# Hybrid decoder layer on one Trainium2 core: operand sums on VectorE alone and over four buffers, gate additions issued behind weight sums, and a new order for the last up-projection unit and the accumulators

## The chip, the cores and the metric

The kernel runs on one NeuronCore of a Trainium2 chip. The metric is the device time of one execution in microseconds. The kernel before took 2260.38 us, the median of three runs (2256.8 to 2262.14).

## The reference, cut to what matters

```python
h = rms_norm(x, norm_mix_g)
proj = h @ w_in                       # q, k, v, gates of three branches
y_m = sigmoid(mo) * rms_norm(mlstm_chunkwise(...))      # branch M
y_d = diff_attention(...)                               # branch D
y_c = memory_cross_attention(cq, mem, ...)              # branch C
g_m, g_d, g_c = split(sigmoid(h @ w_gate + b_gate), 3)
merged = g_m * (y_m @ w_proj_m) + g_d * (y_d @ w_proj_d) + g_c * (y_c @ w_proj_c)
x = x + merged @ w_out
h2 = rms_norm(x, norm_mlp_g)
x = x + square(relu(h2 @ w_up)) @ w_down
```

There are 1024 positions, a width of 1024 and a hidden width of 4096, all in float32. The change concerns the last five lines: the three branch projections with their gates, the output projection and the MLP.

## The kernel before

**First half.** The norm of x, branch C, branch M and branch D are computed one after the other, and the gate columns in pieces between and beside them. A gate step is three matmuls. Each branch writes its result y to device memory, and the gates go there too (line 474).

**Matrix products.** Every product is three matmuls of a high and a low part of the two operands (`mm3`): a source is split into `hi`, a cast on ScalarE, and `lo`, the source less that, on VectorE.

**The stream.** From `stream()` on, the three branch projections, the up and the down projection run as Strassen-Winograd products: a block of weights (four pieces) is summed to seven by four additions on GpSimd (`wino_s`, tiles `wraw`), then split (`wo`); a block of operands (four pieces) is summed to seven in the same way (`wino_t` or `x_fold`), then split (`xo`); seven products of them, 21 matmuls of 128x512, make one weight step n; four steps accumulate in seven PSUM banks and make a round. The steps are numbered through: 0 to 15 are branch C (four rounds), 16 to 31 branch M, 32 to 47 branch D, 48 to 59 the output projection (plain products, tiles `po`), 60 to 123 the up projection (16 rounds, units u), 124 to 187 the down projection (16 rounds p). There are eight banks and a round takes seven, so the first product of a round uses the free one and each later product waits until a sum of the round before has read its bank. These sums (`sums`: one copy on ScalarE, seven additions on VectorE into `c11`, `c21`, `u3`, `u2`, shown as c and u) make the four output blocks.

**Order.** In the stream ScalarE, VectorE, GpSimd and SyncE run in the order of the program text. After each step `side(n)` issues `w_next(n + 3)`, which is the weight sums of what was loaded last (GpSimd), the next weight loads (SyncE) and the split of weight n + 3 (ScalarE, VectorE), and then all that the table `todo` holds for step n, in the order of its list. So whatever waits holds up all that is behind it on its engine.

**Operand sums ahead of the stream.** `x_jobs` (lines 1141 to 1170) makes the operands of branches C, M and D from their y: a job is a pair of rows of blocks and makes two items; an item loads half a tile `xj` (two loads, SyncE), makes three sums on VectorE and one on GpSimd (line 1137), and stores the result to `xtC_d`, `xtM_d` or `xtD_d`, or splits it at once. It is a generator, advanced once per gate step: it waits `wait[0]` steps between the load of an item and the sums of the item before, and `wait[1]` steps up to the store. Three jobs run beside the 64 gate steps between M and D, with waits (4, 5); nine run beside the 96 gate steps ahead of the stream, with waits (3, 4) and three buffers; what is left when the gate steps end is issued behind them. The stream starts with loads of two more operand tiles (`xo`) of branch C.

**Gates.** `fetch` loads a gate block (`gl`), `gate` multiplies (1 + gate) by an output block on VectorE, and GpSimd adds the product to the merged block `mg` (branch M) or the other way about (branch D). In branch M blocks 1, 3 and 2 are done at the round's end n and block 0 at n + 1 or n + 2, since it comes after the load of its gate. The blocks c11, c21 and the gates share a ring of five buffers.

**The second norm** is computed within the first up rounds: `rstd` issues small matmuls (`px`) into the free bank at three points, given by `mid`. `use_up` applies the norm, ReLU and square to an up round's blocks (VectorE, two ScalarE activations for each of four blocks); `up_rest` makes their operand sums (`xts`) and `up_store` stores them (`r_d`). **Down rounds** accumulate in 28 tiles `acc`, loaded with x at step 126 from `x_d`, which lie over the memory of pools closed before (`accum`).

Of the kernel before, what the change touches and what calls it, by code (L numbers as in the profile page):

```python
# [71 lines left out]
class Layer:  # L72
# [1068 lines left out]
    def x_jobs(self, pool, jobs, wait):  # L1141

        V, G = self.nc.vector, self.nc.gpsimd
        items = [(s, kp, slice(c, c + 256)) for s, kp in jobs for c in (0, 256)]
        tiles = []
        for i in range(len(items) + 1):
# [9 lines left out]
            if i:  # L1156
                s, kp, c = items[i - 1]
                r = tiles.pop(0)
                x = self.X[s, kp] if s == "C" and kp < 2 else None
                if x is not None:  # L1160
                    self.split(x[:, 0, 0:3, c], x[:, 1, 0:3, c], r[:, 1:4])
                self.wino_t(r, r, V, G)
            for _ in range(wait[1]):
# [150 lines left out]
    def stream(self):  # L1314
# [33 lines left out]
        def gate(s, u, cs, *order):  # L1348
            for i in order:
                t, k = tg[i], (2 * u + i // 2, i % 2)  # L1350
                if s == "C":
                    mg[k] = mlp.tile([P, 512], F32, tag="ml", name=self.name("mg"))
                V.scalar_tensor_tensor(
                    out=mg[k] if s == "C" else t, in0=t, scalar=1.0, in1=cs[i], op0=ALU.add, op1=ALU.mult
                )
                if s == "M":
                    G.tensor_add(mg[k], mg[k], t)
                elif s == "D":
                    (V if u == 3 else G).tensor_add(t, mg[k], t)
# [60 lines left out]
        for r in range(12):  # L1420
            s, u = "CMD"[r // 4], r % 4
            ps = run(r, (0, 1, 2, 3), s, n)
            n += 4
            cs = sums(ps, four())
            if s == "D":
                if u < 3:
                    gate(s, u, cs, 1, 3, 2, 0)
                    side(n)
                    todo.setdefault(n + 1, []).insert(0, lambda u=u: operands(u, 1, 3, 2, 0))
                continue  # L1430
            m = n + 2 if u == 3 else n
            todo.setdefault(m, []).insert(0, lambda s=s, u=u, cs=cs: gate(s, u, cs, 1, 3, 2))
            m = max(m, n + 1)
            todo.setdefault(m, []).insert(m > n + 1, lambda s=s, u=u: fetch(s, u, 0))
            todo.setdefault(m + 1, []).insert(0, lambda s=s, u=u, cs=cs: gate(s, u, cs, 0))
            side(n)
        self.w_next(n + 3)
        extra.close()
        T["hj"] = R("mhj", his, 2)
        gate("D", 3, cs, 1)  # L1440
        operands(3, 1)
        fetch("D", 3, 0)
        gate("D", 3, cs, 3, 2)
        operands(3, 3, 2)
        gate("D", 3, cs, 0)
        operands(3, 0)
        left.close()
# [11 lines left out]
        def result(u, ps):  # L1459
            x = T["x"]  # L1460
            b = T["b"] = T["o"].tile([P, 4, 512], F32, tag="o", name=self.name("h2"))
            for i in range(4):
                s = slice(i % 2 * 512, (i % 2 + 1) * 512)
                V.scalar_tensor_tensor(out=x[:, i], in0=ps[i], scalar=0.5, in1=x[:, i], op0=ALU.mult, op1=ALU.add)
                v = R_MLP + 2 * u + i // 2
                A.activation(b[:, i], x[:, i], AF.Copy, scale=self.vec[:, v : v + 1])
                if u == 0 and i < 2:
# [11 lines left out]
        for g in range(4):  # L1479
            ps = [pw.tile([P, 512], F32, tag=f"p{4 * (g % 2) + i}", name=self.name("po")) for i in range(4)]  # L1480
            for c in range(3):
# [7 lines left out]
                if c < 2:  # L1489
                    side(n)  # L1490
            result(g, ps)
            if g == 3:
# [29 lines left out]
        next(rs)  # L1522
        mid = {(62, 3): rs.send, (63, 3): rs.send, (64, 2): rs.send}

# [13 lines left out]

        def up_store():
            S.dma_start(*T["rd"])  # L1540

        for u in range(16):
            m = 126 if u == 15 else 64 + 4 * u + (u == 0)
            at(m, up_rest, u)
            at(m + (u < 15), up_store)
        at(110, self.x_load, "N", 0)
# [11 lines left out]
        def accum():  # L1558
            left.close()
            lp = L("acc")  # L1560
            accs.extend(lp.tile([P, 512], F32, name=f"acc{i}") for i in range(28))

# [7 lines left out]
        for u in range(16):  # L1570
# [6 lines left out]
            else:  # L1577
                todo.setdefault(64 if u == 0 else 125, []).insert(0, lambda u=u, cs=cs: use_up(u, cs))
            for f in todo.pop(n, []):
# [69 lines left out]
    def run(self):  # L1649
        tc, nc = self.tc, self.nc  # L1650
        with ExitStack() as ctx:
# [22 lines left out]
            with ExitStack() as c1:  # L1674
# [143 lines left out]
```

## Time and profile before

| What | Value |
|---|---|
| median of 3 runs | 2260.38 us (2256.8 to 2262.14) |
| the profiled execution | 2260.53 us |
| its span, first to last instruction | 2258.8 us |
| mean granted TensorE clock | 0.983 |
| TensorE busy | 95% of the span |
| VectorE, ScalarE, GpSimd busy | 67%, 45%, 26% |
| stream begins | at 1221.48 us |

The profile comes from one execution. A row of a timeline gives the start, the duration, the engine, the operation with its output and inputs, how many were merged, and in brackets the idle time before and what ended it. A row of waits gives the total, how often, and the longest. A row of the windows gives the stretch, its length, busy time with the number of instructions of each engine (TensorE, its weight loads, VectorE, ScalarE, GpSimd), the granted TensorE clock, the mean busy share of the 16 DMA engines, and GB/s. Line 67 is the helper through which the stream issues all its instructions, and line 93 the one for matmuls, so the tiles' names tell what an instruction is. PE is TensorE, DVE VectorE, ACT ScalarE, POOL GpSimd, SP SyncE.

### The profile page before, as it was taken

What the parts mean: (1) busy time and instruction counts of PE and PEld (TensorE: products, weight loads), DVE (VectorE), ACT (ScalarE), POOL (GpSimd) and SP (SyncE); (2) the same over time, 40 slices, a digit from 0 to 9 for tenths busy, and PEclk for the clock granted to TensorE, in tenths of its full rate; (3) what the DMA queues carried; (4) which work ended last, traced back from release to release, by engine and by line L of the source; (5) the groups of instructions that cost most, each with busy time, mean ns of one, the idle gap of its engine ahead of it and who ended that gap; (6) DMA issues with size and microseconds to landing.
All of it is one profiled execution on the core that took longest, in us unless ns stands there. A gap on an engine that the chain in (4) does not pass through costs nothing. (4 is left out here: it accounts for less than half of the span.)

```text
span 2258.8 us, 30482 instructions
## 1 busy us (share of the span) xinstructions
PE 2156.7 (95%) x10953; PEld 1841.5 (82%) x10953; DVE 1516.9 (67%) x2764; ACT 1021.1 (45%) x1995; POOL 591.1 (26%) x568
## 2 busy tenths in 40 slices
PE   7999999999999999999998899899999999699998
PEld 5888888988899999999876667678778887588886
DVE  6643565655347777777644787986688877666687
ACT  6543455444246666665531332324344445443332
POOL 2100000000111111111022347742544434344441
PEclk9999999999999999999999899899999999899999
DMA  7023222121643333333349555334244455554433
GB/s 245 29 85 108 64 83 80 43 71 38 221 117 89 94 89 86 86 85 89 86 148 297 201 182 185 136 103 145 78 145 154 154 186 184 222 200 154 154 137 143
DMA packets 138398, 293.51 MB, mean 130 GB/s; under 512 B 13793, under 2 KB 44806, under 8 KB 132486
## 3 DMA queue, kind: packets, MB, share of 16 engines
q1 hardware_dynamic: 135942, 278.98, 37.9%
q10 hardware_dynamic: 2304, 12.58, 1.4%
q8 instruction: 86, 1.41, 0.3%
q14 instruction: 66, 0.54, 0.1%
HBM read 192.91 MB, written 73.43 MB: 118 GB/s over the span
## 5 line engine op out<-in xcount | busy, mean ns | idle before, releaser
L93 PE MATMUL p<-xo,wo 128*128 128x512 f32 x3696 | 873.8, 398 | 63.4 <-ACT xo L67 22.2
L93 PEld LDWEIGHTS p<-xo,wo 128*128 128x128 f32 x3696 | 703.0, 192 | 232.6 <-ACT xo L67 23.8
L93 PE MATMUL mm<-w,hT 128*128 128x384 f32 (+3 forms) x2496 | 472.2, 331 | 8.9 <-DVE dsg L114 5.5
L67 POOL TENSOR_TENSOR wraw<-wraw 128x256 f32<-128x256 f32 x352 | 374.9, 1076 | 358.0 <-DMA wraw<-in_wdown 148.1
L93 PE MATMUL mm<-hT,w 128*128 128x512 f32 x1920 | 466.4, 395 | 1.9 <-ACT gt L473 1.2
L93 PEld LDWEIGHTS mm<-hT,w 128*128 128x128 f32 x1920 | 353.2, 188 | 77.1 <-ACT gt L473 2.4
L93 PEld LDWEIGHTS mm<-w,hT 128*128 128x128 f32 x2496 | 388.2, 189 | 22.8 <-DVE dsg L114 7.7
L67 ACT CAST wo<-wraw 128x896 fp32r<-128x896 f32 (+1 forms) x186 | 171.2, 931 | 445.2 <-PE p L93 222.5
L67 DVE TENSOR_TENSOR wo<-wraw,wo 128x896 fp32r<-128x896 f32 (+1 forms) x186 | 232.1, 1254 | 171.0 <-ACT wo L67 170.3
L114 DVE TENSOR_TENSOR w<-raw,w 128x256 fp32r<-128x256 f32 (+3 forms) x272 | 130.5, 502 | 60.2 <-ACT w L113 59.4
L1009 ACT ACTIVATE dpe<-sc,dst,drr 128x256 f32<-128x256 f32 (+7 forms) x128 | 106.6, 833 | 99.8 <-DVE dst L1005 91.1
L113 ACT CAST w<-raw 128x256 fp32r<-128x256 f32 (+3 forms) x272 | 121.5, 469 | 66.2 <-PE mm L93 26.3
L67 DVE TENSOR_TENSOR xo<-xo 128x1536 fp32r<-128x1536 f32 (+1 forms) x58 | 127.1, 2207 | 20.8 <-ACT xo L67 19.8
L129 POOL TENSOR_SCALAR hss<-hss 128x4 f32<-128x4 f32 x8 | 3.3, 408 | 414.4 <-ACT mscr L754 273.1
L67 ACT CAST xo<-xo 128x1536 fp32r<-128x1536 f32 (+1 forms) x58 | 97.0, 1691 | 25.7 <-DMA xo<-y 21.4
L1001 DVE CUSTOM_DVE_ANT_0 sc<-sc,tmask 128x256 f32<-128x256 f32 (+7 forms) x128 | 97.1, 758 | 12.7 <-PE sc L93 12.6
L67 DVE TENSOR_TENSOR u<-u,p 128x512 f32<-128x512 f32 x140 | 93.8, 686 | 12.7 <-DVE c L67 0.9
L93 PE MATMUL sc<-dk,dq 128*128 128x512 f32 (+3 forms) x384 | 90.3, 343 | 0.0
L129 POOL TENSOR_SCALAR drr<-drr 128x16 f32<-128x16 f32 x16 | 3.3, 204 | 313.4 <-DVE drr L955 313.4
L93 PE MATMUL po<-mh,wo 128*128 128x512 f32 x256 | 79.0, 389 | 0.0
L93 PE MATMUL po<-dv,daT 128*128 128x256 f32 x576 | 75.2, 274 | 0.5 <-DVE daT L114 0.5
L93 PEld LDWEIGHTS po<-dv,daT 128*128 128x128 f32 x576 | 74.0, 189 | 1.6 <-DVE daT L114 0.9
(267 smaller groups left out, 2450.9 us busy)
## 6 DMA issues: line engine op xcount, KB each, us to landing
xo<-r_d SPq DMA_DIRECT2D x19, 1024.0 KB, 6.7
dk<-dsg SPq DMA_DIRECT2D x64, 256.0 KB, 4.4
wraw<-in_wup SPq DMA_DIRECT2D x64, 256.0 KB, 3.5
r_d<-xts SPq DMA_DIRECT2D x16, 1024.0 KB, 4.4
wraw<-in_wdown SPq DMA_DIRECT2D x64, 256.0 KB, 4.0
xo<-r_d SPq DMA_DIRECT2D x19, 768.0 KB, 4.4
raw<-in_wgate SPq DMA_DIRECT2D x48, 256.0 KB, 3.2
gates<-gt SPq DMA_DIRECT2D x48, 256.0 KB, 3.3
```

Source lines behind the costliest of these rows:

```text
L67: return self.tc.keep_in_program_order(f(*a, **k))
L93: self.pin(self.nc.tensor.matmul(out, l, r, start=start, stop=stop))
L113: nc.scalar.copy(hi, src)
L114: nc.vector.tensor_sub(lo, src, f32(hi))
L129: g.tensor_scalar(r, ss, 1.0 / width, EPS, op0=ALU.mult, op1=ALU.add)
L1001: V.tensor_tensor_reduce(out=sc[:, 0:n], in0=sc[:, 0:n], in1=self.tmask[:, D - n : D], scale=1.0, scalar=-3.0e38, op0=ALU.add, op1=ALU.max ...
L1009: nc.scalar.activation(pe[c][:, 0:n], sc[:, 0:n], AF.Exp, bias=t8[:, 2 + c : 3 + c], scale=rr[:, i, c : c + 1], accum_out=t8[:, 4 + c : 5 ...
```

## The change

1. `x_jobs` makes all four sums of an item on VectorE (`x_fold`). One M job moves from the last gate stage to the one between M and D (8 and 16 items now instead of 6 and 18). The waits become (3, 4) in the former and (2, 4) in the latter, which has four buffers instead of three.
2. The additions behind the gates become a function of their own (`adds`). In branch M (rounds 0 to 2) they are issued one step after the gate product, behind the weight sums of that step, and block 0's gate load, product and addition one step later than before. In branch D (rounds 0 to 2) the gate product is issued behind the weight split of its step instead of ahead, the addition one step later, and the split of the merged block (`operands`) at the third step instead of the first.
3. In the output projection, four casts come ahead of four squares, and `w_sums` is called ahead of `result`.
4. The second and third point of the norm's small matmuls move from steps (63, 3) and (64, 2) to (64, 0) and (64, 4); unit 0's `use_up` and `up_rest` come one step later.
5. Unit 15's `use_up` comes behind the operand split of step 125 instead of ahead, its `up_store` is issued from GpSimd instead of SyncE, and the 28 accumulators lie in reverse order in memory, so that the first round's seven lie over pools closed long before rather than over the buffers of `xts`.

```diff
-                self.wino_t(r, r, V, G)
+                self.x_fold(r, r, V)
...
-                if s == "M":
-                    G.tensor_add(mg[k], mg[k], t)
-                elif s == "D":
+        def adds(s, u, *order):
+            for i in order:
+                t, k = tg[i], (2 * u + i // 2, i % 2)
+                if s == "M":
+                    G.tensor_add(mg[k], mg[k], t)
+                else:
                     (V if u == 3 else G).tensor_add(t, mg[k], t)
...
+            put = lambda m, f, *x: todo.setdefault(m, []).insert(0, lambda: f(*x))
             if s == "D":
                 if u < 3:
-                    gate(s, u, cs, 1, 3, 2, 0)
+                    put(n + 3, operands, u, 1, 3, 2, 0)
+                    put(n + 1, adds, s, u, 1, 3, 2, 0)
+                    put(n, gate, s, u, cs, 1, 3, 2, 0)
                     side(n)
-                    todo.setdefault(n + 1, []).insert(0, lambda u=u: operands(u, 1, 3, 2, 0))
                 continue
+            late = s == "M" and u < 3
             m = n + 2 if u == 3 else n
-            todo.setdefault(m, []).insert(0, lambda s=s, u=u, cs=cs: gate(s, u, cs, 1, 3, 2))
-            m = max(m, n + 1)
-            todo.setdefault(m, []).insert(m > n + 1, lambda s=s, u=u: fetch(s, u, 0))
-            todo.setdefault(m + 1, []).insert(0, lambda s=s, u=u, cs=cs: gate(s, u, cs, 0))
+            if s == "M":
+                put(m + late, adds, s, u, 1, 3, 2)
+            if u == 3:
+                todo.setdefault(m, []).insert(s == "M", lambda s=s, u=u: fetch(s, u, 0))
+            else:
+                at(n + 1 + late, fetch, s, u, 0)
+            put(m, gate, s, u, cs, 1, 3, 2)
+            e = m + 1 if u == 3 else n + 2 + late
+            if s == "M":
+                put(e, adds, s, u, 0)
+            put(e, gate, s, u, cs, 0)
             side(n)
...
-        mid = {(62, 3): rs.send, (63, 3): rs.send, (64, 2): rs.send}
+        mid = {(62, 3): rs.send, (64, 0): rs.send, (64, 4): rs.send}
...
-            m = 126 if u == 15 else 64 + 4 * u + (u == 0)
+            m = 126 if u == 15 else 64 + 4 * u + 2 * (u == 0)
             at(m, up_rest, u)
-            at(m + (u < 15), up_store)
+            at(m + (u < 15), up_store, S if u < 15 else G)
...
-            accs.extend(lp.tile([P, 512], F32, name=f"acc{i}") for i in range(28))
+            accs.extend([lp.tile([P, 512], F32, name=f"acc{i}") for i in range(28)][::-1])
...
-                todo.setdefault(64 if u == 0 else 125, []).insert(0, lambda u=u, cs=cs: use_up(u, cs))
+                at(65 if u == 0 else 125, use_up, u, cs)
...
-                        jobs = self.x_jobs(xj, [("C", 2), ("C", 3), ("M", 0)], (4, 5))
+                        jobs = self.x_jobs(xj, [("C", 2), ("C", 3), ("M", 0), ("M", 1)], (3, 4))
...
-                    with tc.tile_pool(name="pgh", bufs=2) as self.gpool, tc.tile_pool(name="xjd", bufs=3) as xj:
-                        jobs = self.x_jobs(xj, [("C", 0), ("C", 1)] + [(s, k) for s in "MD" for k in range(s == "M", 4)], (3, 4))
+                    with tc.tile_pool(name="pgh", bufs=2) as self.gpool, tc.tile_pool(name="xjd", bufs=4) as xj:
+                        jobs = self.x_jobs(xj, [("C", 0), ("C", 1)] + [(s, k) for s in "MD" for k in range(2 * (s == "M"), 4)], (2, 4))
```

On SyncE, at the end of the last gate stage and the start of the stream, the order before is this (`gates<-gt` stores a gate block, `xj<-y` are the two loads of an item, `xtD_d<-xj` is an item's store, `xo` the operand tile of C 2):

```order
L474 DMA gates<-gt_2160_13014 128x512
L67 DMA xtD_d<-xj_2156_12962 512x1x256
L67 DMA xj_2161_13022<-y1 128x2x256 x2
L67 DMA xtD_d<-xj_2159_12995 512x1x256
L67 DMA xj_2162_13030<-y1 128x2x256 x2
L67 DMA xtD_d<-xj_2161_13022 512x1x256
L67 DMA xj_2163_13038<-y1 128x2x256 x2
L67 DMA xtD_d<-xj_2162_13030 512x1x256
L67 DMA xj_2164_13046<-y1 128x2x256 x2
L67 DMA xtD_d<-xj_2163_13038 512x1x256
L67 DMA xo_2165_13112<-y2 128x1024
L67 DMA xtD_d<-xj_2164_13046 512x1x256
```

The operand tile's last part, `xo<-xtC_d`, stands right behind these. At the same place, from the last weight loads on, the order is now:

```order
L67 DMA xj_2160_12994<-y1 128x2x256 x2
L474 DMA gates<-gt_2161_13010 128x512
L67 DMA xtD_d<-xj_2154_12955 512x1x256
L67 DMA xj_2163_13024<-y1 128x2x256 x2
L474 DMA gates<-gt_2164_13046 128x512
L67 DMA xtD_d<-xj_2160_12994 512x1x256
L67 DMA xo_2165_13112<-y2 128x512
L67 DMA xtD_d<-xj_2163_13024 512x1x256
L67 DMA xo_2165_13112<-y2 128x1024
L67 DMA xo_2165_13112<-xtC_d 128x2048
```

No item load stands behind the last gate store any more; two item stores do.

On GpSimd, from the end of branch M's first round on, the order before is this (`wraw` are four weight sums, `mg<-mg,gl` a gate addition):

```order
L67 TENSOR_TENSOR mg_13262<-mg_13262,gl_13829 128x512
L67 TENSOR_TENSOR mg_13264<-mg_13264,gl_13831 128x512
L67 TENSOR_TENSOR mg_13266<-mg_13266,gl_13833 128x512
L67 TENSOR_TENSOR wraw_13868<-wraw_13868 128x2x128 x4
L67 TENSOR_TENSOR mg_13332<-mg_13332,gl_13915 128x512
L67 TENSOR_TENSOR wraw_13938<-wraw_13938 128x2x128 x4
```

And now, at the same place:

```order
L67 TENSOR_TENSOR wraw_13868<-wraw_13868 128x2x128 x4
L67 TENSOR_TENSOR mg_13262<-mg_13262,gl_13829 128x512
L67 TENSOR_TENSOR mg_13264<-mg_13264,gl_13831 128x512
L67 TENSOR_TENSOR mg_13266<-mg_13266,gl_13833 128x512
L67 TENSOR_TENSOR wraw_13936<-wraw_13936 128x2x128 x4
L67 TENSOR_TENSOR mg_13332<-mg_13332,gl_13946 128x512
```

Each group of additions now has one more group of weight sums ahead of it.

On VectorE, at step 125, the order before is this (`c` and `u` are unit 15's blocks times the norm, the `xo` rows the two parts of an operand's split):

```order
L67 TENSOR_TENSOR c_2844_18018<-c_2844_18018,rb 128x512
L67 TENSOR_TENSOR c_2845_18019<-c_2845_18019,rb 128x512
L67 TENSOR_TENSOR u_2846_18020<-u_2846_18020,rb 128x512
L67 TENSOR_TENSOR u_2847_18021<-u_2847_18021,rb 128x512
L67 TENSOR_TENSOR xo_18040<-xo_18040 128x1536
L67 TENSOR_TENSOR xo_18040<-xo_18040 128x2048
L67 TENSOR_TENSOR wo_18151<-wraw_18030,wo_18151 128x896
```

And now:

```order
L67 TENSOR_TENSOR xo_18040<-xo_18040 128x1536
L67 TENSOR_TENSOR xo_18040<-xo_18040 128x2048
L67 TENSOR_TENSOR c_2844_18018<-c_2844_18018,rb 128x512
L67 TENSOR_TENSOR c_2845_18019<-c_2845_18019,rb 128x512
L67 TENSOR_TENSOR u_2846_18020<-u_2846_18020,rb 128x512
L67 TENSOR_TENSOR u_2847_18021<-u_2847_18021,rb 128x512
L67 TENSOR_TENSOR wo_18151<-wraw_18030,wo_18151 128x896
```

The split of the operand of step 127 stands ahead of unit 15's four products, on VectorE and in the same way on ScalarE.

More of the change, by code (lines that the diff above doesn't have):

```diff
@@ L1141, in x_jobs @@
     def x_jobs(self, pool, jobs, wait):
-        V, G = self.nc.vector, self.nc.gpsimd
+        V = self.nc.vector
         items = [(s, kp, slice(c, c + 256)) for s, kp in jobs for c in (0, 256)]
@@ L1439, in stream @@
         T["hj"] = R("mhj", his, 2)
[L1440 to L1446, printed above, removed]
+        for i in ((1,), (3, 2), (0,)):
+            gate("D", 3, cs, *i)
+            adds("D", 3, *i)
+            operands(3, *i)
+            if 1 in i:
+                fetch("D", 3, 0)
         left.close()
@@ L1462, in result @@
             for i in range(4):
-                s = slice(i % 2 * 512, (i % 2 + 1) * 512)
                 V.scalar_tensor_tensor(out=x[:, i], in0=ps[i], scalar=0.5, in1=x[:, i], op0=ALU.mult, op1=ALU.add)
@@ L1466, in result @@
                 A.activation(b[:, i], x[:, i], AF.Copy, scale=self.vec[:, v : v + 1])
+            for i in range(4):
+                s = slice(i % 2 * 512, (i % 2 + 1) * 512)
                 if u == 0 and i < 2:
@@ L1490, in stream @@
                     side(n)
+            self.w_sums()
             result(g, ps)
@@ L1537, in up_rest, with up_store @@
             T["rd"] = self.rd[u, :, 3:7], t
-        def up_store():
-            S.dma_start(*T["rd"])
+        def up_store(q):
+            q.dma_start(*T["rd"])
         for u in range(16):
-            m = 126 if u == 15 else 64 + 4 * u + (u == 0)
+            m = 126 if u == 15 else 64 + 4 * u + 2 * (u == 0)
             at(m, up_rest, u)
-            at(m + (u < 15), up_store)
+            at(m + (u < 15), up_store, S if u < 15 else G)
         at(110, self.x_load, "N", 0)
```

## The prediction

> **What bounds the kernel now.** I read the page's engine table first, then the clock row, then who PE waits for in the half that the change touches, then timelines around the longest waits.
>
> ```profile
> span 2258.8 us, 30482 instructions
> PE 2156.7 (95%) x10953; PEld 1841.5 (82%) x10953; DVE 1516.9 (67%) x2764; ACT 1021.1 (45%) x1995; POOL 591.1 (26%) x568
> ```
>
> PE is busy 95% of the span, so nothing can be won but PE's idle time and its slow clock. The waits of PE from 1150 us to the end:
>
> ```profile
> PE p L93 <- ACT xo L67: 22.2, 3, 15.0
> PE p L93 <- DVE c L67: 15.9, 8, 3.4
> PE p L93 <- DVE acc L67: 8.1, 1, 8.1
> PE p L93 <- DVE xo L67: 8.0, 6, 3.2
> PE px L93 <- DVE u L67: 3.6, 1, 3.6
> PE p L93 <- DVE wo L67: 3.6, 3, 1.3
> ```
>
> Some 56 us in few pieces: operands (xo), the sums that free PSUM banks (c), one accumulator (acc). The change aims at three of them. Where PE stood still long, its clock is half behind the gap; windows of an undisturbed place and of two behind such gaps (PEclk is the third figure from the right, the DMA share follows):
>
> ```profile
> 1190.00:1221.00 31.00, 31.00 (x138) 25.69 (x137) 11.67 (x27) 4.60 (x8) 5.21 (x7) 1.00 0.97 310
> 1235.00:1255.00 20.00, 5.01 (x9) 2.90 (x10) 9.05 (x13) 6.07 (x5) 1.44 (x2) 0.50 0.88 305
> 1417.00:1423.00 6.00, 6.00 (x16) 4.66 (x17) 5.55 (x8) 4.12 (x3) 2.30 (x4) 0.54 0.47 175
> ```
>
> So a gap costs more than itself: behind one of 3.35 us (at 1416.80, below) PE made 16 matmuls in 6 us at clock 0.54; at the undisturbed 138 in 31 us it would be 27. The 11 missing are some 2.5 us.
>
> **Term 1, start of the stream.** PE has 42 matmuls ready at 1221.48 and then waits for the operand tile of C 2:
>
> ```profile
> 1221.48 9.68 PE L93 MATMUL p<-xo,wo 128*128 128x512 f32 x42
> 1246.20 0.79 PE L93 MATMUL p<-xo,wo 128*128 128x512 f32 x1 [15.04 <-ACT xo L67]
> 1248.00 2.50 PE L93 MATMUL p<-xo,wo 128*128 128x512 f32 x5 [1.00 <-DVE xo L67]
> 1251.75 0.80 PE L93 MATMUL p<-xo,wo 128*128 128x512 f32 x1 [1.26 <-ACT xo L67]
> 1254.08 8.12 PE L93 MATMUL p<-xo,wo 128*128 128x512 f32 x25 [1.53 <-DVE xo L67]
> ```
>
> The gaps are 15.04 + 3.8 (1.00, 1.26, 1.53). The clock adds 4.9: seven matmuls take 1254.08 - 1246.20 - 3.8 = 4.1 us instead of 7 x 0.225 = 1.6, the next 25 take 8.12 instead of 5.7. The start costs 23.8. The tile was late because SyncE issues in program order, and four item loads (first and last here), with stores that wait for their sums, stood ahead:
>
> ```profile
> 1222.44 0.33 SPq L474 DMA_DIRECT2D gates<-gt  x1
> ...
> 1224.91 1.65 SPq L67 DMA_DIRECT2D xj<-y  x2
> ...
> 1236.17 1.72 SPq L67 DMA_DIRECT2D xj<-y  x2
> ...
> 1243.89 0.63 SPq L67 DMA_DIRECT2D xo<-xtC_d  x1
> ```
>
> The loads come every (1236.17 - 1224.91)/3 = 3.75 us; the tile's second half is issued 22.4 us after the stream began. The tile view gives VectorE's sum and POOL's, one in four, that moves to VectorE:
>
> ```profile
> L1136 DVE TENSOR_TENSOR xj<-xj x18: 412/425/953, 1165.5 to 1240.6; 128x256 f32<-128x256 f32 x18
> L1137 POOL TENSOR_TENSOR xj<-xj x18: 722/734/1655, 1166.2 to 1241.6; 128x256 f32<-128x256 f32 x18
> ```
>
> After the change 16 items instead of 18, each over 6 gate steps instead of 7: 16 x 6 = 96, so all loads stand ahead of the last gate store, and only the last two stores stand between it and the tile. How early it comes, three ways. Two items fewer alone: 2 x 3.75 = 7.5 us. If the DMA engines bind (share 0.97 from 1190 on), what counts is the work left at 1190: two items fewer, and one more done ahead (96 steps of three matmuls, 3 x 0.225 us, began at 1156.7; the 49 up to 1190 make 8 items at 6, 7 at 7), 3 x 3.75 = 11 us. By the program's order alone the tile follows the last item load by 7.7 us as before (1236.17 to 1243.89), and that load now comes 6 steps, 4 us, before the stream: issue 4 to 8 us behind its start, 14 to 18 us earlier. The first gap is 15.04 less what is gained, at least nothing; the three small gaps (3.8) stay, and of the slow clock's 5 about half stays while a gap of over 3 us is left. At 14 earlier: 23.8 - (1.0 + 3.8 + 2.5) = 16.5 less; at 11: 11 + 1 = 12 less; at 7.5: 7.5. I take **-15**, between the second and the third, since a fourth buffer takes waits off SyncE; bounds -7.5 and -20 (all but the small gaps). POOL's sum of 0.73 becomes one of 0.42 on VectorE, without a handover: 0.3 us per item, inside these bounds. VectorE's fourth sum per item lies beside PE, which did not wait in 1190 to 1221 (31.00 busy of 31).
>
> **Term 2, the gate additions.** At the end of the M rounds PE waits for the sum c:
>
> ```profile
> 1392.22 20.01 PE L93 MATMUL p<-xo,wo 128*128 128x512 f32 x81 [3.27 <-DVE c L67]
> ...
> 1416.80 22.05 PE L93 MATMUL p<-xo,wo 128*128 128x512 f32 x84 [3.35 <-DVE c L67]
> 1441.58 3.23 PE L93 MATMUL p<-xo,wo 128*128 128x512 f32 x9 [2.73 <-DVE c L67]
> ```
>
> From one of these waits to the next are 24.58 and 24.78 us for a round of 84 matmuls, which undisturbed take 84 x 0.225 = 18.9: 5.8 us of loss a round, gap and slow clock together, three times; and the three waits for wo (3.6 above) fall in the D rounds. At stake are some 20 us.
>
> VectorE was late with c since it waited for a weight cast, which waited for POOL's weight sums, which stood behind additions that wait for the gate product:
>
> ```profile
> 1384.83 1.09 DVE L67 TENSOR_TENSOR wo<-wraw,wo 128x896 fp32r<-128x896 f32 x1 [3.93 <-ACT wo L67]
> ...
> 1407.94 1.09 DVE L67 TENSOR_TENSOR wo<-wraw,wo 128x896 fp32r<-128x896 f32 x1 [5.19 <-ACT wo L67]
> ...
> 1410.56 5.58 DVE L67 TENSOR_TENSOR xo<-xo 128x1536 fp32r<-128x1536 f32 x2
> ```
> ```profile
> 1398.44 5.47 POOL L67 TENSOR_TENSOR mg<-mg,gl 128x512 f32<-128x512 f32 x3 [4.79 <-DVE gl L67]
> 1403.87 3.07 POOL L67 TENSOR_TENSOR wraw<-wraw 128x256 f32<-128x256 f32 x4
> ...
> 1411.76 6.47 POOL L67 TENSOR_TENSOR wraw<-wraw 128x256 f32<-128x256 f32 x4
> ```
>
> With the weight sums first, they no longer wait 4.79 + 5.47 us for the gate: VectorE's 3.93 and 5.19 go, and c comes earlier by that much, until something else is last. At 1416 and 1441 two splits of xo (5.58) stand on VectorE right ahead of c and stay; at 1392 only one. So I count two thirds of the first loss, 4, one third of the other two, 2 each, and 3 of the 3.6 for wo, which in D rounds is put ahead of the gates: **-11**. Bounds: -3 (wo alone) and -17 (a small gap of 1 us a round is left). Additions themselves are no cheaper: their cover is POOL's idle time, 74% of the span.
>
> The trace has a price for crowding: four weight sums take 3.07 us where VectorE waited, 6.47 beside the splits of xo. The Trainium skill, SBUF — State Buffer, "Who interferes with whom", has a rule against this term: a VectorE operation with two SBUF operands and a GpSimd operation that reads SBUF lock each other out for the whole instruction, so reordering saves none of that work. By that rule the term would be near nothing; the two rows agree with it as far as they go, and that is rival 1.
>
> **Term 3, the norm's small products.** The second of them sits in PE's order behind two products of step 64 and waits for the last sum:
>
> ```profile
> 1624.55 2.08 PE L93 MATMUL px<-dg,ones 128*128 128x128 f32 x8 [3.60 <-DVE u L67]
> ```
>
> Now the first of them sits behind one product of step 64, the second behind five, and the first takes a bank that the same sum frees. PE arrives with 6 more matmuls left behind (6 x 0.23 = 1.4, at half clock more), and what the first product no longer holds up at step 63 is swallowed by the wait for the same sum: **+1.4**, bounds -1 and +3.
>
> **Term 4, before and in the first down round.**
>
> ```profile
> 1941.94 0.80 PE L93 MATMUL p<-xo,wo 128*128 128x512 f32 x1 [5.92 <-ACT xo L67]
> 1960.13 10.14 PE L93 MATMUL p<-xo,wo 128*128 128x512 f32 x33 [8.14 <-DVE acc L67]
> ```
> ```profile
> 1939.89 0.63 ACT L67 ACTIVATE rq<-u 128x512 f32<-128x512 f32 x1
> 1940.43 3.25 ACT L67 CAST xo<-xo 128x1536 fp32r<-128x1536 f32 x2
> ```
> ```profile
> 1949.13 4.43 DMA r_d<-xts
> ...
> 1954.42 4.24 DMA acc<-x_d
> ```
>
> ScalarE ran eight gate activations of unit 15 before casting the operand: now the cast comes first, 4.8 us earlier (from 1940.43 to about 1935.7) and most of the slow clock behind the 5.92 us gap: some 7 at step 127. The accumulators waited for the store of xts (4.43), since the first lay over its buffer, and then 4.24 for their load; now they lie over memory that is free before, and the load no longer waits for the store. VectorE's order remains: xts, then the first accumulator. Xts ended at 1949.1 (where its store begins); it moves back a little behind the activations. So the 1960.13 becomes 1950 to 1952. What PE wins at step 127 it would wait for at 128, so the later end alone counts: **-9**, bounds -6 and -11. The unit's last store goes to POOL's queue; nothing rereads that row for tens of steps: 0.
>
> **Without price.** While the items ran from 1190 to 1221, PE was busy all 31.00 us, so the one job more in the middle gate stage costs 0, 1 at most. Squares behind casts, w_sums ahead of result (POOL's order stays the same), D's last group in one loop: 0.
>
> **Sum.** -15 - 11 + 1.4 - 9 = -33.6, from the profiled execution's 2260.53 (span 2258.8 and 1.7 around it), which is within 0.2 us of the median 2260.38. That is **2227**.
>
> **Rivals.** (1) Term 2 gives nothing, since the port's work is the same: 2238. For it: 6.47 against 3.07. Against: VectorE stood idle 3.93 and 5.19 there, no lock. (2) The start is bound by DMA, only the two items count: 2260.5 - 7.5 - 18.6 = 2234. For it: share 0.97. (3) The other side: in the M rounds the last addition moves one step back, to one step before the next round's sums. It holds the buffer that sum c21 takes, and stands on POOL behind weight sums that wait for their load:
>
> ```profile
> 1421.84 7.58 POOL L67 TENSOR_TENSOR wraw<-wraw 128x256 f32<-128x256 f32 x4 [3.62 <-DMA wraw<-in_wpd]
> ```
> ```profile
> L67 DVE TENSOR_TENSOR c<-u,p 128x512 f32<-128x512 f32 x56 | 38.2, 683 | 4.9 <-POOL mg L67 2.0
> ```
>
> If it comes later than c21 can be made, VectorE waits with PE behind it, in three rounds, each with 2.5 us of slow clock. With term 2 lost the rest is -22.6, so it decides from 22.6/3 - 2.5 = 5 us late a round; 8 us late gives 2260.5 - 22.6 + 3 x 10.5 = 2269. For it: that load was waited for 3.62 us, and 7.58 for the sums behind it. Against: in all rounds c waited 2.0 us for POOL's mg. (4) The end gives only 6, as the accumulators stay late: 2230.
>
> **Chances.** Forecast 0.48 (own range 2219 to 2236), rival 1 0.20, rival 2 0.18, rival 4 0.09, rival 3 0.05 (half of it beyond 2260). Rivals 1 and 2 together give 2245. Range 2213 to 2247: below, start -20, additions -15, end -11. About 4.5 us (0.2%) is what a measurement can tell. Faster 0.94, same 0.02, slower 0.04.
>
> **What would show it.** Right: PE's first gap under 4 us and the tile's load issued under 10 us after the stream's start; no wait of PE for c over 1.5 us at the end of the first M round; the acc wait gone or under 2 us; px waiting about 4 us. Wrong: PE waits for xo at the start by 10 us or more; VectorE's idle before wo stays at 4 to 5 us in M rounds; a new wait c <- POOL mg; POOL's wraw idle grows.

## The result, and the profile after

The changed kernel took 2250.44 us, the median of nine runs (2244.77 to 2255.14), beside 2260.63 us for the kernel before on the same chip. The ratio is 0.9945 with a 95% interval of 0.9931 to 0.9960: 12 us faster, between 9 and 16. The forecast was 2227 with a range of 2213 to 2247, so the sign was right, but little more than a third of the 33.6 us came. The profiled execution took 2247.84 us with a span of 2245.8, which is 13.0 us under the span before.

TensorE's waits from 1150 us to the end, in the changed kernel:

```profile
PE p L93 <- DVE c L67: 19.7, 9, 7.7
...
PE p L93 <- ACT acc L67: 3.2, 1, 3.2
PE mm L93 <- ACT w L113: 3.1, 1, 3.1
...
PE p L93 <- ACT xo L67: 2.9, 1, 2.9
PE p L93 <- DVE acc L67: 2.6, 1, 2.6
```

The wait for xo by ScalarE fell from 22.2 us to 2.9 and the one for the accumulators from 8.1 to 5.8. The wait for c, which the second term was to shorten, rose from 15.9 to 19.7, and there is a wait for a gate weight (`w`) of 3.1 us that before did not have. Where these lie is best seen by the start of the weight steps in the two traces. Each step is 21 matmuls of `p<-xo,wo`, and both traces hold all of them, so the starts can be counted off:

| Stretch (weight steps) | before | after | difference in the stretch |
|---|---|---|---|
| up to the stream's start, step 0 | 1221.48 | 1229.36 | +7.9 |
| steps 0 to 2 (start) | 1259.51 | 1252.97 | -14.4 |
| steps 3 to 20 | 1353.04 | 1346.63 | +0.1 |
| steps 21 to 24 | 1372.09 | 1369.73 | +4.1 |
| steps 25 to 28 | 1397.11 | 1389.83 | -4.9 |
| steps 29 to 32 | 1422.97 | 1418.31 | +2.6 |
| steps 33 to 46 | 1502.45 | 1492.83 | -5.0 |
| steps 47 to 64 (output projection, norm's products) | 1631.17 | 1624.18 | +2.6 |
| steps 65 to 68 | 1651.46 | 1646.87 | +2.4 |
| steps 69 to 124 | 1926.30 | 1922.14 | +0.4 |
| steps 125 to 128 (unit 15, accumulators) | 1966.03 | 1952.76 | -9.1 |

The times are those at which the stretch ends, that is, at which the next step starts; the last column is the stretch's length after less before. What the change won at the start and at the end is what was forecast; five other stretches gave 20 us back, where 1.4 were forecast.

**Ahead of the stream.** TensorE around the stream's start, after:

```profile
1211.24 18.28 PE L93 MATMUL mm<-hT,w 128*128 128x512 f32 x72 [3.15 <-ACT w L113]
1229.36 9.68 PE L93 MATMUL p<-xo,wo 128*128 128x512 f32 x42
1241.92 0.51 PE L93 MATMUL p<-xo,wo 128*128 128x512 f32 x1 [2.88 <-ACT xo L67]
1243.71 2.93 PE L93 MATMUL p<-xo,wo 128*128 128x512 f32 x6 [1.29 <-DVE xo L67]
```

The gap of 15.04 us at the start is 2.88 now. But in the last gate stage TensorE stands still for 3.15 us, and 72 matmuls behind it take 18.28 us where 16.2 would do. ScalarE, which casts the gate weight, and SyncE, which loads it:

```profile
1210.78 0.71 ACT L113 CAST w<-raw 128x256 fp32r<-128x256 f32 x2 [7.35 <-DMA raw<-in_wgate]
```
```profile
1200.56 1.61 SPq L67 DMA_DIRECT2D xj<-y  x2
...
1204.24 1.66 SPq L67 DMA_DIRECT2D xj<-y  x2
1205.94 0.68 SPq L443 DMA_DIRECT2D raw<-in_wgate  x1
...
1235.42 0.94 SPq L67 DMA_DIRECT2D xo<-xtC_d  x1
```

The last gate weight is loaded at 1205.94, behind item loads and stores, and lands 4.8 us later. Before, it was issued here:

```profile
1187.48 0.33 SPq L443 DMA_DIRECT2D raw<-in_wgate  x1
```

Not all of the +7.9 belongs to it. Matched one by one, the matmul right ahead of this wait starts 2.8 us later than before, the one behind it 6.1 and the stream 7.9, so the gate weight and the slow clock behind it cost 5.1. Some 1.3 come right behind the middle gate stage, where branch D starts with a wait that the trace before does not have:

```profile
631.45 8.79 PE L93 MATMUL mm<-w,hT 128*128 128x384 f32 x49 [1.54 <-DVE dv L114]
```

The other 1.5 lie ahead of that, where traces of the same code differ by as much.

**Branch M's rounds.** TensorE, and the gate products on VectorE that end its waits:

```profile
1364.58 24.01 PE L93 MATMUL p<-xo,wo 128*128 128x512 f32 x96 [2.14 <-DVE c L67]
1389.02 16.66 PE L93 MATMUL p<-xo,wo 128*128 128x512 f32 x72 [0.43 <-DVE u L67]
1413.33 20.78 PE L93 MATMUL p<-xo,wo 128*128 128x512 f32 x84 [7.66 <-DVE c L67]
```
```profile
1363.23 0.69 DVE L67 SCALAR_TENSOR_TENSOR gl<-gl,u 128x512 f32<-128x512 f32 x1 [4.36 <-DMA gl<-gates]
...
1407.05 0.69 DVE L67 SCALAR_TENSOR_TENSOR gl<-gl,u 128x512 f32<-128x512 f32 x1 [5.40 <-DMA gl<-gates]
1407.66 5.02 DVE L67 TENSOR_TENSOR xo<-xo 128x1536 fp32r<-128x1536 f32 x2
1412.61 0.67 DVE L67 TENSOR_TENSOR c<-u,p 128x512 f32<-128x512 f32 x1
```

The first of the three waits that the prediction named (3.27 at 1392) is gone, but there is a new one of 2.14 at step 24, the second grew from 3.35 to 7.66, and VectorE now waits 4.36 and 5.40 us for the load of block 0's gate, and c stands behind that.

**Norm and end.** TensorE again:

```profile
1604.51 6.68 PE L93 MATMUL p<-xo,wo 128*128 128x512 f32 x22 [1.76 <-DVE wo L67]
...
1615.47 2.08 PE L93 MATMUL px<-dg,ones 128*128 128x128 f32 x8 [4.28 <-DVE u L67]
...
1642.31 3.34 PE L93 MATMUL p<-xo,wo 128*128 128x512 f32 x12 [2.15 <-DVE c L67]
```
```profile
1932.66 1.67 PE L93 MATMUL p<-xo,wo 128*128 128x512 f32 x6 [0.61 <-DVE xo L67]
...
1942.33 1.65 PE L93 MATMUL p<-xo,wo 128*128 128x512 f32 x3 [3.18 <-ACT acc L67]
1946.56 9.80 PE L93 MATMUL p<-xo,wo 128*128 128x512 f32 x30 [2.59 <-DVE acc L67]
```

The gap of 5.92 us before step 127 is 0.6, and the one of 8.14 is two of 3.18 and 2.59. A wait for c at 1642 is new. The wait for wo, in step 62, was 1.00 before; it makes this step 0.8 us longer.

### The profile page after: what moved, and what is told of

Read it like the earlier page. It is cut to its first block, busy times and chain, and to the rows that moved or that the text cites. A ratio compares the mean times of both kernels' runs of the same rounds, so it can differ in the third digit from the quotient of the medians.

```text
span 2245.8 us, 30420 instructions
## 1 busy us (share of the span) xinstructions
PE 2158.6 (96%) x10953; PEld 1844.0 (82%) x10953; DVE 1522.1 (68%) x2788; ACT 1020.8 (45%) x1995; POOL 570.0 (25%) x545
## 5 line engine op out<-in xcount | busy, mean ns | idle before, releaser
L93 PE MATMUL p<-xo,wo 128*128 128x512 f32 x3696 | 873.2, 398 | 43.4 <-DVE c L67 19.7
L67 POOL TENSOR_TENSOR wraw<-wraw 128x256 f32<-128x256 f32 x352 | 363.3, 1043 | 459.6 <-DMA wraw<-in_wdown 141.1
```

Of the source, the lines that this page charges most:

```text
L67: return self.tc.keep_in_program_order(f(*a, **k))
L93: self.pin(self.nc.tensor.matmul(out, l, r, start=start, stop=stop))
```

## The experiments

All were timed against the kernel before; a ratio times 2260.5 gives the microseconds. Each trace is one execution, and stretches of the same code differ between traces by 1 to 2 us.

### The four parts alone

Each is the kernel before with one part of the change. The third point of the change, the order in the output projection, has no run of its own. The first:

```diff
-                self.wino_t(r, r, V, G)
+                self.x_fold(r, r, V)
...
-                        jobs = self.x_jobs(xj, [("C", 2), ("C", 3), ("M", 0)], (4, 5))
+                        jobs = self.x_jobs(xj, [("C", 2), ("C", 3), ("M", 0), ("M", 1)], (3, 4))
...
-... name="xjd", bufs=3 ... for k in range(s == "M", 4)], (3, 4))
+... name="xjd", bufs=4 ... for k in range(2 * (s == "M"), 4)], (2, 4))
```

> Of the change only the operand sums ahead of the stream (all four on VectorE, eight and sixteen items, four buffers). Theory: the last gate weight's load now stands on SyncE behind two more item loads, TensorE waits for it by about 3 us in the last gate stage and the stream begins some 7 to 8 us later than before; its start then loses 9 to 10 us instead of 23.8. Net 6 to 7 us faster. Rival (the blind prediction): the stream begins where it did, and the time falls by about 15 us; the late start of the stream then comes from another part of the change.

It took 2251.47 us, ratio 0.9957 (0.9944 to 0.9971): 10 us faster, between 7 and 13.

```profile
1210.42 18.46 PE L93 MATMUL mm<-hT,w 128*128 128x512 f32 x72 [3.19 <-ACT w L113]
1228.72 9.68 PE L93 MATMUL p<-xo,wo 128*128 128x512 f32 x42
1239.91 0.50 PE L93 MATMUL p<-xo,wo 128*128 128x512 f32 x1 [1.50 <-ACT xo L67]
```

The wait for the gate weight and the late start of the stream (1228.72) belong to this part alone. At step 3 the trace is 9.1 us ahead of the kernel before. The theory's mechanism stands; its 6 to 7 us lie at the lower end of the interval and below the 9.1 of the trace. The prediction's 15 are inside neither. Which edit of this part puts the gate weight's load behind the items (the waits, the fourth buffer, the job moved) no run tells.

The second is the edit of `adds`, `gate`, `fetch` and `operands` as the diff of the change shows it.

> Of the change only the gate additions and operands of branches M and D. Theory: the weight sums come earlier, but block 0's gate load now stands on SyncE behind an operand tile, VectorE waits for it by 4 to 5 us in two rounds, and new waits for c take back most: a net gain of 2 to 4 us. Rival (the blind prediction): 11 us faster. Second rival (the shared port): no change at all, 0 within 1 us.

It took 2257.97 us, ratio 0.9992 (0.9983 to 1.0000): between 4 us faster and nothing. The prediction's 11 falls, and neither the theory's 2 to 4 nor the second rival's nothing is excluded by the time. In the trace the losses move from round to round: steps 21 to 24 are 6.9 us longer than before, steps 25 to 28 5.8 shorter, steps 29 to 32 2.9 longer. In sum steps 21 to 46 are 2.7 us longer there, though this execution, at 2264.39 us, was the slowest of the eleven. VectorE waits 6.84 and 4.88 us for gl:

```profile
1374.58 0.69 DVE L67 SCALAR_TENSOR_TENSOR gl<-gl,u 128x512 f32<-128x512 f32 x1 [6.84 <-DMA gl<-gates]
...
1417.84 0.69 DVE L67 SCALAR_TENSOR_TENSOR gl<-gl,u 128x512 f32<-128x512 f32 x1 [4.88 <-DMA gl<-gates]
```

The third:

```diff
-        mid = {(62, 3): rs.send, (63, 3): rs.send, (64, 2): rs.send}
+        mid = {(62, 3): rs.send, (64, 0): rs.send, (64, 4): rs.send}
...
-            m = 126 if u == 15 else 64 + 4 * u + (u == 0)
+            m = 126 if u == 15 else 64 + 4 * u + 2 * (u == 0)
...
-                todo.setdefault(64 if u == 0 else 125, []).insert(0, lambda u=u, cs=cs: use_up(u, cs))
+                if u == 0:
+                    at(65, use_up, u, cs)
+                else:
+                    todo.setdefault(125, []).insert(0, lambda u=u, cs=cs: use_up(u, cs))
```

> Of the change only the later points of the norm's small matmuls and unit 0's steps. Theory: the wait of the first small product for the last sum is the same, with more products left behind, and unit 0's norm falls into the round end at step 68: 4 to 5 us slower. Rival (the blind prediction): 1.4 us slower. Second rival: within 1 us, the loss seen there comes from other parts.

It took 2263.32 us, ratio 1.0017 (1.0008 to 1.0026): 4 us slower, between 2 and 6, as the theory had it; the prediction's 1.4 lies just outside. In the trace steps 65 to 68 are 2.4 us longer than before, as in the changed kernel, and steps 63 and 64 1.1.

The fourth is unit 15's order, the store from GpSimd and the reversed accumulators.

> Of the change only unit 15's order, its store from GpSimd and the reversed accumulators. Theory and blind prediction agree: 9 us faster, of which 8 at step 127, and 1 at step 128, where TensorE waits for two accumulators in turn instead of one. Rival: the accumulators alone carry it, step 127 then stays as before and step 128 falls by 8.

It took 2250.76 us, ratio 0.9959 (0.9946 to 0.9971): 9 us faster, between 7 and 12. In its trace 7.5 us are won by the start of step 128 and 2.0 in it, as the theory and the prediction had it, so the rival falls. The four parts alone add up to -17 us, the change as a whole to -12, each with some 3 to 5 us of uncertainty, so the sum agrees with the whole as far as this can tell.

### The queue on SyncE: two loads moved forward

Both are the changed kernel with one line edited. Block 0's gate load goes to the head of its step:

```diff
-                at(n + 1 + late, fetch, s, u, 0)
+                put(n + 1 + late, fetch, s, u, 0)
```

> The changed kernel, but block 0's gate load goes ahead of the operand tile's loads of the same step instead of behind. Theory (the load that stands behind 1.75 MB of operands holds up VectorE, and c behind it): VectorE's waits for gl of 4.36 and 5.40 us go, the waits for c at steps 24 and 32 fall from 2.3 and 7.8 us to under 1 and about 3, and the time falls by 6 to 9 us against the changed kernel, to about 2243. Rival (the shared port: the same work, only elsewhere): c is no earlier, 2250 as the changed kernel.

It took 2243.87 us, ratio 0.9931 (0.9914 to 0.9948). Against the changed kernel's 0.9945 that alone would not settle it; the trace does. TensorE in the same rounds:

```profile
1342.20 35.90 PE L93 MATMUL p<-xo,wo 128*128 128x512 f32 x156 [0.42 <-DVE u L67]
1379.20 2.55 PE L93 MATMUL p<-xo,wo 128*128 128x512 f32 x9 [1.10 <-DVE c L67]
...
1403.76 3.37 PE L93 MATMUL p<-xo,wo 128*128 128x512 f32 x12 [3.04 <-DVE c L67]
```

156 matmuls pass step 24 without a wait, VectorE's two waits for gl are gone, and step 32's 7.66 are 3.04, as expected. Against the changed kernel steps 21 to 24 are 3.8 us shorter and steps 29 to 32 5.0. But steps 25 to 28 are 2.5 longer and steps 33 to 46 5.9: TensorE comes earlier to rounds in which c is late for other reasons, and waits there. From step 21 to step 46 only 0.4 us are left of the 8.8 in this trace (2.7 in that of the mended kernel below). So the load is the cause of these two waits, and not of the rounds' whole loss. The rest by which this run is ahead lies before step 21 and behind step 128, where the edit changes nothing. So the 2243 us came out, but not by the 6 to 9 us that were expected of this load, and that part is luck.

For the gate weight, a fourth buffer lets its load go earlier in SyncE's order:

```diff
-... tc.tile_pool(name="rpg", bufs=3, reuse_waits="tile") as self.rp:
+... tc.tile_pool(name="rpg", bufs=4, reuse_waits="tile") as self.rp:
```

> The changed kernel with four buffers instead of three for the raw gate weights, so that the last load stands six item loads earlier on SyncE. Theory (SyncE's order): TensorE's wait of 3.15 us in the last gate stage goes, the stream begins 4 to 5 us earlier, the operand tile is issued again about 6 us behind that, and the time falls by 4 to 5 us against the changed kernel, to 2246. Rival (the transfers bind): the tile's load is issued no earlier than now (1235.4 us), the first gap of the stream grows by what is won ahead of it, and the time stays at 2250.

It took 2241.20 us, ratio 0.9915 (0.9900 to 0.9931): 19 us under the kernel before, 7 under the changed one. TensorE and SyncE:

```profile
1183.11 38.61 PE L93 MATMUL mm<-hT,w 128*128 128x512 f32 x169 [0.81 <-DVE w L114]
1221.55 9.68 PE L93 MATMUL p<-xo,wo 128*128 128x512 f32 x42
1236.36 0.79 PE L93 MATMUL p<-xo,wo 128*128 128x512 f32 x1 [5.13 <-ACT xo L67]
```
```profile
1183.08 0.33 SPq L443 DMA_DIRECT2D raw<-in_wgate  x1
...
1230.63 0.94 SPq L67 DMA_DIRECT2D xo<-xtC_d  x1
```

169 matmuls run without a gap and the stream begins at 1221.55, as it did before the change. The tile's load is issued 9.1 us behind that, 4.8 earlier than in the changed kernel, but not 6.1 behind as there: the first gap grows from 2.88 to 5.13. So the rival holds in part, SyncE's order in the main. Of 7.8 us at the stream's start 8.0 are left at step 3, since less slow clock stands behind: 22 matmuls are busy 7.17 us from 1236 to 1245 here (clock 0.68), and 9.29 from 1241 to 1253 in the changed kernel (0.57). The wait of 3.15 us and the slow clock behind it are 5.1 of the 7.8, and the wait for dv at the start of branch D is gone too. That is why more came than the 4 to 5 us of the theory.

### The norm, taken apart

> The changed kernel with the norm's points and unit 0's steps as before. Theory: 3 to 5 us faster than the changed kernel, 2246, with the losses from step 62 to 69 at 12 us instead of 17. Rival (the parts lean on each other): no difference, 2250.

This is the changed kernel with the third part undone. It took 2245.24 us, ratio 0.9936 (0.9923 to 0.9949), 2 us better by the ratio and 5 by the medians; by time alone that is not clear of the changed kernel. In the trace steps 65 to 68 are 2.4 us shorter and steps 62 to 64 0.7. Step 62 stays 0.8 us longer than before, as in every trace built on the changed kernel and in none of a single part.

> The kernel before with the second and third point of the norm's small matmuls moved, unit 0's use_up and up_rest as before. Theory: the two moves of this part cost separately, the matmuls' points about 2 us at steps 62 to 65, unit 0's later steps the 2.4 us at step 68, so 2 us slower than before. Rival: all of the loss hangs on the points, 4 us slower.

This is the kernel before with `mid` changed and nothing else. It took 2262.84 us, ratio 1.0006 (0.9996 to 1.0015), not distinguishable from no change. TensorE:

```profile
1625.26 2.08 PE L93 MATMUL px<-dg,ones 128*128 128x128 f32 x8 [7.16 <-DVE u L67]
```

One wait of 7.16 us stands in place of 0.92 and 3.60, and its stretch is 2.2 us longer; steps 65 to 68 are as before. So the two moves cost separately, as the first theory had it, and the rival's 4 us are outside the interval. Unit 0's later steps cost 2.4 in every trace that has them. The points cost 1 to 2 (+1.1 to +2.3 in steps 63 and 64 of the five traces with them), but the same stretch lies between -1.8 and +1.2 in the traces without, so their price is not sharp.

### The end, taken apart

> The kernel before with only unit 15's activations behind the operand split of step 125. Theory (the later end counts): step 127 gains 8 us, but step 128 waits for the accumulators' loads up to the time as before or later, so nothing is won, 0 to 2 us. Rival: both gaps count by themselves, 6 to 8 us faster.

```diff
-                todo.setdefault(64 if u == 0 else 125, []).insert(0, lambda u=u, cs=cs: use_up(u, cs))
+                if u == 0:
+                    todo.setdefault(64, []).insert(0, lambda u=u, cs=cs: use_up(u, cs))
+                else:
+                    at(125, use_up, u, cs)
```

It took 2260.57 us, ratio 0.9999 (0.9991 to 1.0008): nothing, as the theory had it.

```profile
1936.76 1.67 PE L93 MATMUL p<-xo,wo 128*128 128x512 f32 x6 [0.79 <-DVE xo L67]
...
1950.20 1.65 PE L93 MATMUL p<-xo,wo 128*128 128x512 f32 x3 [6.96 <-ACT acc L67]
1960.00 6.29 PE L93 MATMUL p<-xo,wo 128*128 128x512 f32 x17 [8.15 <-DVE acc L67]
```

The 5.92 us at step 127 go, and come back as 6.96 at step 128, where 8.15 follow as before.

> The kernel before with only the accumulators in reverse order. Theory: step 127 waits as before (5.9 us), the accumulators' loads start before the store of the unit's sums, and step 128 gains the 4 to 5 us of that load: 4 to 6 us faster. Rival: the first accumulator stays behind the unit's sums on VectorE and nothing is won, 0 to 1 us.

```diff
-            accs.extend(lp.tile([P, 512], F32, name=f"acc{i}") for i in range(28))
+            accs.extend([lp.tile([P, 512], F32, name=f"acc{i}") for i in range(28)][::-1])
```

It took 2259.04 us, ratio 0.9991 (0.9982 to 1.0001): nothing, or up to 4 us faster.

```profile
1939.48 0.79 PE L93 MATMUL p<-xo,wo 128*128 128x512 f32 x1 [6.06 <-ACT xo L67]
...
1955.85 10.36 PE L93 MATMUL p<-xo,wo 128*128 128x512 f32 x33 [6.98 <-DVE acc L67]
```

Each alone wins 0 to 2 us, both together 9. The theory's 4 to 6 us for the accumulators were not met (in the trace steps 125 to 128 are 1.3 us shorter); its rival comes nearer: the first accumulator is on VectorE behind the unit's own sums, and these come no earlier.

### All that was mended, and one step more

> The three edits of the runs beside it together. Theory: they add up, 15 us below the changed kernel, 2235. Rival (transfers bind at the start): 10 us below, 2240.

This is the changed kernel with both loads moved forward and the norm's part undone. It took 2232.70 us, ratio 0.9881 (0.9865 to 0.9897): 27 us under the kernel before, 14 under the changed one. By the ratios the three edits alone gave 7, 3 and 2, so they add up as far as this can tell, and the rival's 2240 is outside the interval.

> The kernel with three mended edits (2232.7 us), and branch M's gate additions of rounds 0 to 2 on VectorE instead of GpSimd. Theory (the shared port is what is left: beside additions on GpSimd of 5.47 us for three, two weight splits on VectorE took 4.27 us instead of 2.16): without them the splits run at 1.08 each, the additions cost 0.7 each on VectorE, about as much as they took from it, and weight sums and the ring's buffers come earlier: steps 24 to 36 lose 2 to 5 us less. Rival (VectorE is the late engine there, the lock costs it little): twelve additions of 0.7 us more stand ahead of c, 2 to 4 us slower than the mended kernel.

```diff
-                    G.tensor_add(mg[k], mg[k], t)
+                    (V if u < 3 else G).tensor_add(mg[k], mg[k], t)
```

It took 2230.48 us, ratio 0.9868 (0.9852 to 0.9883), which the time does not tell from the mended kernel. VectorE, branch M's first round:

```profile
1346.95 1.08 DVE L67 TENSOR_TENSOR wo<-wraw,wo 128x896 fp32r<-128x896 f32 x1
1347.95 1.88 DVE L67 TENSOR_TENSOR mg<-mg,gl 128x512 f32<-128x512 f32 x3
```

Three additions take 1.88 us here and GpSimd took 5.47 to 5.92 for them, with VectorE's two splits beside them stretched from 1.08 each to 4.27 in all, as this row of the changed kernel shows:

```profile
1394.13 4.27 DVE L67 TENSOR_TENSOR wo<-wraw,wo 128x896 fp32r<-128x896 f32 x2
```

In these rows VectorE spends about as much on the additions as it lost beside them. Over all of steps 21 to 32 it spends less, as the windows show, the mended kernel first:

```profile
1342.27:1409.21 66.94, 61.61 (x254) 48.81 (x252) 58.16 (x51) 22.34 (x21) 48.24 (x35) 0.95 0.58 204
...
1344.18:1406.76 62.58, 59.36 (x253) 48.28 (x252) 53.12 (x61) 22.33 (x21) 25.75 (x26) 0.97 0.60 219
```

VectorE is busy 53.12 us with ten additions more, and 58.16 without. The stretch is 4.4 us shorter than in the mended kernel and 2.8 shorter than with the gate load put first (65.35), which is the 2 to 5 us of the theory; with one trace of each, and 1.6 us between the two that lack the edit, it is not shown. Both of the kernels of this section beat the two compared; they are the best that was run.

## Why the prediction was wrong

**Term 1, -15: right in its own stretch, -14.4, with a price beside it that was set at nothing.** The first gap (2.88) and the tile's issue 6.1 us behind the start came as worked out; the small gaps shrank from 3.8 to 1.8 instead of staying. The step that failed is the sentence that VectorE's sum and the items lie beside TensorE, "which did not wait in 1190 to 1221 (31.00 busy of 31)". A stage without a wait shows that nothing in it was late at the old pace, and not what a faster pace beside it costs. The items' loads and stores share SyncE's queue with the loads of the gate weights, and the last of these moved 18 us back in time, behind five item stores and five item loads (from 1188.94 to 1204.24). That cost 5.1 us, and the run with the fourth buffer shows it as the cause. The prediction's "0, 1 at most" for the job more in the middle gate stage was 1.3, with the wait for dv. The list of SyncE's order ahead of the prediction begins 17 us behind that gate weight's load, with the item load at 1223.16, so it does not show it.

**Term 2, -11: -3.2 in steps 21 to 46, and -2 alone.** The mechanism was there: the wait at 1392 went, since the weight sums no longer stand behind the gate additions. The step that failed is "until something else is last": it named the splits of xo and left out the load of block 0's gate, which the change also moves. It now stands on SyncE behind an operand tile of 1.75 MB, issued at 1398.64 in the trace and landed 8.3 us later, and VectorE waits for it ahead of c. The run with the load put first shows this as the cause at steps 24 and 32, and shows too that most of what it frees is waited for in later rounds: the bound that the term was worked out from was one of several of nearly the same height. The prediction also misread the waits for wo: two (1.28 and 1.30) lie in the D rounds, the third (1.00) in step 62 of the up projection, where it grew. Rival 1 (the same work at a shared port) is not excluded. Alone, the part won nothing that is clear of the interval, as this rival says. The losses that moved with the gate's load are another cause beside it. With that load put first, steps 21 to 46 are 3.6 us shorter than before, in the mended kernel 5.9, and there with the additions off GpSimd 10.7, which is about the 11 that were forecast; each is one trace. Rival 3's wait came too, at a small size: in the groups of instructions from 1250 to 1935 us c's wait for GpSimd's additions rose from 2.0 to 4.8 us in all:

```profile
L67 DVE TENSOR_TENSOR c<-u,p 128x512 f32<-128x512 f32 x56 | 38.3, 683 | 7.5 <-POOL mg L67 4.8
```

**Term 3, +1.4: +2.6 from step 47 to 64, and +2.4 that were not counted.** The wait of about 4 us came (4.28). Steps 63 and 64, where the products are, are 1.4 us longer in this trace, as forecast, which is partly luck, since that stretch scatters by more. The rest of the 2.6 are 0.8 in step 62 and 0.4 in the output projection, which the prediction had at 0: no run tells which edit they come from, and that it is the third point of the change, which was never run alone, is likely but not shown. The step that failed in the term itself is unit 0's norm: moved one step back it was treated as free, and it made c late at step 68.

**Term 4, -9: -9.1.** Right, and for the reason given: what is won at step 127 is waited for at step 128, and only both edits together move the later end. The accumulators' loads are issued at 1930.33 now, ahead of the unit's sums, and were issued at 1949.56, behind their store. That the remaining wait is under 2 us was not met (3.18 and 2.59): ScalarE's copy of the first accumulator now stands behind unit 15's activations.

The sum of the terms, with what each measured, is +7.9 - 14.4 - 3.2 + 5.0 - 9.1 = -13.8, and 0.8 in between makes the 13.0 of the spans. Rival 2 (only the two items count at the start, -7.5) is not met in its stretch, but that the transfers bind may hold in part: with the gate weight's load in its place the tile is issued 9.1 us behind the start instead of 6.1, where the DMA engines' share is 1.00 from 1190 to 1221:

```profile
1190.00:1221.00 31.00, 31.00 (x138) 25.66 (x138) 14.46 (x35) 4.61 (x8) 0.00 (x0) 1.00 1.00 320
```

What stays open: why steps 33 to 46, branch D in the main, gained 5.0 us in the changed kernel and 1.3 in the run of the second part alone. The waits for wo go in both, but in the latter two waits of 1.22 for c come in their place. Nothing tried here tells why, nor how much of term 2 the shared port kept.

## What to carry to other kernels

When instructions are moved, follow each of their loads through the queue that issues it: twice here a small load came to stand behind other loads and something waited for it, and putting one of the two right gave 7 us. A stage without waits is no proof that more work beside it is free; look at what else its queue carries. Where two waits follow each other closely, take both away or neither: each alone won nothing that the time tells, both together 9 us.

## What was not expected of the hardware

A load of 256 KB landed 8.3 us after its issue when 1.75 MB had been issued just ahead of it on the same queue (1398.64), and 4.1 us when it went first (issued at 1391.76). The Trainium skill, DMA: Bandwidth & Descriptors, section "Two DMAs through the same engine are not ordered", has the descriptors of one queue on one DMA engine starting in order; the two landings agree with that.

TensorE's granted clock fell behind gaps shorter than the 3.35 us of the prediction's window: behind the 3.15 us in the gate stage it was 0.66 from 1211 to 1216 (third figure from the right), and 0.54 behind the 2.88 us at the stream's start, with a further gap of 1.29 in the window:

```profile
1211.00:1216.00 5.00, 4.76 (x14) 3.55 (x15) 2.87 (x8) 1.18 (x3) 0.00 (x0) 0.66 0.57 198
...
1242.00:1246.00 4.00, 2.71 (x6) 1.93 (x7) 2.86 (x2) 3.13 (x3) 0.00 (x0) 0.54 1.01 416
```
